# Storing split weights once and loading the parts again in the dense streams of a decoder trunk

## The chip, the cores and the metric

The kernel runs on one core of a Trainium2 chip. The metric is device time of one execution in microseconds (us). TensorE (PE) does the matmuls and has two clock levels, 1.2 and 2.4 GHz; VectorE (DVE), ScalarE (ACT) and GpSimd (POOL) do the elementwise work; SyncE (SP) issues nearly all transfers, in order, on one queue that 16 DMA engines serve. Each engine runs its own instructions strictly in the order that was fixed when the program was built.

## The reference

The reference is a decoder trunk of two layers on 2048 tokens of 1024 channels, in float32. Layer 0 mixes tokens with windowed attention, layer 1 with an RWKV-7 recurrence. After each mixer come an output projection and a gated per-layer embedding:

```python
for i in range(DEPTH):
    hn = rms_norm(h, norm_g[i])
    m = swa_sink_mixer(...) if i % 2 == 0 else rwkv7_mixer(...)   # both end in (o * silu(z)) @ w_out
    h = h + m
    h = h + jax.nn.sigmoid(h @ ple_w_gate[i]) * (p[i] @ ple_w_proj[i])
return rms_norm(h, final_norm_g)
```

## The kernel before

To keep float32 accuracy on the matmul path, each operand is split into a rounded part `hi` (ACT, a copy to the type fp32r) and a remainder `lo` (DVE, `src - hi`), by `Trunk.split`. A product is then three matmuls, `hi*hi`, `hi*lo` and `lo*hi` (`mm3`, L567 to L569).

The work is in four phases: `attn_proj` (0 to about 490 us), `attention` (to about 1250), `rwkv_proj` (to about 1985) and `rwkv` (to the end). Beside attention, and beside the recurrence of `rwkv`, runs a dense stream, an object of the class `Dense`. It is a list of jobs (kind, group of 512 tokens), done in order. In attention the jobs are

```python
"00 01 02 03 10 11 o0 g0 o1 l0 g1 o2 l1 g2 o3 l2 g3 12 l3".split()
```

where 00 to 03 and 10 to 12 are the embedding projections p0 and p1 of a group, o the output projection, g the gate and l the low-rank input of the next layer. In `rwkv` they are z0 to z3 (a projection), o0 g0 o1 g1 o2 g2, then p3 o3 g3. A job is cut into units of one weight tile of 128 x 1024 (8 units for o, g and z, 2 for p and l), 86 + 98 = 184 units in all. A unit is 8 steps of 3 matmuls. Between two steps the other work of the phase issues its own instructions, so the stream fills what attention or the recurrence leaves free on TensorE.

For unit u, `w_load` (L110) issues the load of the raw weights, `wraw`, at step 8(u-2), and `w_split` (L120) makes `dwh` on ACT and `dwl` on DVE at step 8(u-1)+4. The matmuls of u begin at step 8u. All these tiles come from one pool, `wp`, with six buffers (L464), so that before the change a unit takes three of them, `wraw`, `dwh` and `dwl`, and two units fit. The same weights come back for every group of tokens: the tile of o0's first unit is loaded and split again for o1, o2 and o3.

The order of the instructions on each engine is not quite that of the code: the program is built with a scheduler that moves instructions by its own timeline (`schedule_with_timeline_sim=True`, L1429).

Of the kernel before, what the change touches and what calls it, by code (L numbers as in the profile page):

```python
# [10 lines left out]
F32R = mybir.dt.float32r  # L11
# [7 lines left out]
KT = C // 128  # L19
# [24 lines left out]
def f32(ap):  # L44
    return ap.bitcast(F32)
# [7 lines left out]
class Dense:  # L53
# [54 lines left out]
        return aux  # L108

    def w_load(self, u):  # L110
        kind, n, c = u
        k = self.kinds[kind]
        kt = k.get("kt", KT)
        m = 128 * KT // kt
        raw = self.tr.wp.tile([128, KT * 128], F32, name="wraw", tag="w4")
        w = k["w"][:, k.get("c0", 0) + c * m:k.get("c0", 0) + (c + 1) * m]
        self.nc.sync.dma_start(out=raw.rearrange("p (k m) -> p k m", m=m), in_=w.rearrange("(k p) m -> p k m", p=128))
        return raw

    def w_split(self, u, raw):  # L120
        hi, lo = (self.tr.wp.tile([128, KT * 128], F32R, name=nm, tag="w4") for nm in ("dwh", "dwl"))
        self.tr.split(hi, lo, raw, scale=self.kinds[u[0]].get("scale"))
        return hi, lo

    def run(self):
        units, begin, events = [], {}, {}

        def at(step, *what):
            events.setdefault(step, []).append(what)

        owner = []
        for j, (kind, n) in enumerate(self.jobs):
            kt = self.kinds[kind].get("kt", KT)
            b = begin[kind, n] = 8 * len(units)
            units += [(kind, n, c) for c in range(self.kinds[kind].get("units", kt))]
            for k in range(kt):
                free = owner[len(owner) - KT] if len(owner) >= KT else -99
                if "after" in self.kinds[kind]:

                    fill = max(free + 1, begin[self.kinds[kind]["after"], n] + 8 * k + 8)  # L140
                else:
                    fill = max(free, b + k - 9) + 3
                    pre = 3 if "pre" in self.kinds[kind] else 0
                    if pre:
                        at(fill - pre, "pre", j, k)
                    at(fill - pre - self.lead, "fetch", j, k)
                assert fill <= b + k
                at(fill, "fill", j, k)
                if (kind, n) == self.late:
                    at(max(fill, b), "late", j, k)  # L150
                owner.append(8 * len(units) - kt + k)
        for u in range(len(units)):
            at(8 * (u - 2), "w_load", u, None)
            at(8 * (u - 1) + 4, "w_split", u, None)
            for ct in range(KT if "aux" in self.kinds[units[u][0]] and not units[u][2] else 0):
                at(8 * (u + ct) - 4, "aux", units[u][:2], ct)
        raws, tiles, wraw, ws, auxs = {}, {}, {}, {}, {}
        job = -1
        first = -16
        assert first <= min(events)  # L160
        yield
        for s in range(first, 8 * len(units)):
            self.left = 8 * len(units) - s
            for what, a, k in sorted(events.pop(s, []), key=lambda e: ("fetch", "w_load", "fill", "pre", "aux", "w_split", "late").index(e[0])):
                if what == "fetch":
                    kind, n = self.jobs[a]
                    kd = self.kinds[kind]
                    while not kd.get("ready", lambda n, k: True)(n, k):
                        yield
                    raws[a, k] = kd["fetch"](n, k)  # L170
                elif what == "fill":
                    kind, n = self.jobs[a]
                    tiles[a, k] = self.kinds[kind].get("fill", self.fill)(n, k, raws.pop((a, k), None))
                elif what == "pre":
                    kind, n = self.jobs[a]
                    raws[a, k] = self.kinds[kind]["pre"](n, k, raws[a, k])
                elif what == "aux":
                    auxs[a, k] = self.kinds[a[0]]["aux"](a[1], k)
                elif what == "late":
                    while self.rest is None:  # L180
                        yield
                    self.tr.split(*(x[:, G - self.rest.shape[2]:] for x in tiles[a, k]), self.rest[:, k])
                elif what == "w_load":
                    wraw[a] = self.w_load(units[a])
                else:
                    ws[a] = self.w_split(units[a], wraw.pop(a))
            if s >= 0:
                u, i = divmod(s, 8)
                kind, n, c = units[u]
                kd = self.kinds[kind]  # L190
                kt = kd.get("kt", KT)
                k, ct = i % kt, c * (KT // kt) + i // kt
                if k == 0:
                    if ct == 0:
                        job += 1
                    ps = self.mp.tile([128, G], F32, name="ps")
                hi, lo = ws[u]
                m = KT // kt * 128
                sl = slice(k * m + (ct % (KT // kt)) * 128, k * m + (ct % (KT // kt)) * 128 + 128)
                self.tr.mm3(ps, hi[:, sl], lo[:, sl], *tiles[job, k], k == 0, k == kt - 1)  # L200
                if k == kt - 1:
                    self.tr.start(kd["evac"](n, ct, ps, tiles[job, ct] if kt == KT else None, auxs.pop(((kind, n), ct), None)))
                    self.cols_done[kind, n] = ct + 1
            yield
# [1228 lines left out]
```

## Time and profile before

| | us |
|---|---|
| median of 3 runs | 3120.83 (3119.34 to 3126.83) |
| the profiled execution | 3124.84, its span 3123.0 |
| PE busy | 2885.0 (92% of the span) |
| DVE busy | 2112.2 (68%) |
| ACT busy | 1438.3 (46%) |
| POOL busy | 1023.5 (33%) |

The span is the time from the first to the last instruction of the profiled execution. An engine's busy time is the union of its instructions; its idle time costs something only where it stands on the way to the end. The transfers moved 532.87 MB, at a mean of 171 GB/s.

### The profile page before, as it was taken

The numbers are of one execution on the slowest core, as the hardware profiler recorded it, in microseconds if no ns is written. First come the engines' busy times: TensorE is split into PE (matmuls) and PEld (weight loads), VectorE is DVE, ScalarE is ACT, GpSimd is POOL, SyncE is SP. The second block draws the span as 40 slices with busy tenths as digits, with TensorE's granted clock in tenths as the row PEclk, the third lists the DMA queues.
The fourth block names the chain that finished last, engine by engine and source line by source line (L and its number), as shares of the span: only waits on it lengthen the run. The fifth ranks groups of instructions, "written<-read, shape, count | busy, mean of one in ns | idle before, by whom it ended". The sixth has DMA issues, their size and how long they took to land. (4 is left out here: it accounts for less than half of the span.)

```text
span 3123.0 us, 56427 instructions
## 1 busy us (share of the span) xinstructions
PE 2885.0 (92%) x21416; PEld 2284.2 (73%) x21416; DVE 2112.2 (68%) x3665; ACT 1438.3 (46%) x2976; POOL 1023.5 (33%) x886
## 2 busy tenths in 40 slices
PE   7999998999999988898999899988989988989997
PEld 5888886777777766686777688766767766767876
DVE  6532434775888766738678966688795686795555
ACT  5311115874675644626667733433334443443433
POOL 2243500002211232404556700214454435435421
PEclk9999999999999999999999899998899999999999
DMA  7665847985675455636556778855657558568463
GB/s 220 184 142 110 172 131 207 248 210 151 170 189 143 145 172 172 194 115 190 180 185 199 214 210 218 236 150 145 145 150 176 126 143 202 116 150 204 122 192 95
DMA packets 704032, 532.87 MB, mean 171 GB/s; under 512 B 255504, under 2 KB 558736, under 8 KB 703760
## 3 DMA queue, kind: packets, MB, share of 16 engines
q1 hardware_dynamic: 696080, 518.76, 60.3%
q0 software_dynamic: 7680, 10.50, 3.1%
q8 instruction: 169, 2.77, 0.4%
q14 instruction: 103, 0.84, 0.1%
HBM read 350.09 MB, written 168.56 MB: 166 GB/s over the span
## 5 line engine op out<-in xcount | busy, mean ns | idle before, releaser
L567 PE MATMUL ps<-dhi,dwh 128*128 128x512 f32 x1472 | 609.8, 416 | 17.0 <-ACT dwh L516 11.7
L569 PE MATMUL ps<-dhi,dwl 128*128 128x512 f32 x1472 | 595.2, 405 | 26.7 <-DVE dwl L518 15.0
L568 PE MATMUL ps<-dlo,dwh 128*128 128x512 f32 x1472 | 594.3, 405 | 8.3 <-DVE dlo L518 6.1
L567 PE MATMUL ps<-xH,wh 128*128 128x512 f32 x1408 | 556.9, 402 | 25.4 <-DVE kb L1049 10.5
L568 PE MATMUL ps<-xL,wh 128*128 128x512 f32 x1408 | 560.7, 399 | 1.8 <-DVE xL L518 1.1
L569 PE MATMUL ps<-xH,wl 128*128 128x512 f32 x1408 | 561.5, 399 | 0.8 <-DVE wl L518 0.8
L569 PEld LDWEIGHTS ps<-dhi,dwl 128*128 128x128 f32 x1472 | 283.2, 192 | 96.0 <-DVE dwl L518 18.9
L567 PEld LDWEIGHTS ps<-dhi,dwh 128*128 128x128 f32 x1472 | 283.0, 192 | 88.1 <-ACT dwh L516 12.7
L567 PEld LDWEIGHTS ps<-xH,wh 128*128 128x128 f32 x1408 | 269.4, 192 | 88.9 <-DVE kb L1049 14.0
L568 PEld LDWEIGHTS ps<-dlo,dwh 128*128 128x128 f32 x1472 | 283.5, 193 | 67.8 <-DVE dlo L518 8.4
L568 PEld LDWEIGHTS ps<-xL,wh 128*128 128x128 f32 x1408 | 270.8, 192 | 62.3 <-DVE xL L518 2.3
L569 PEld LDWEIGHTS ps<-xH,wl 128*128 128x128 f32 x1408 | 269.9, 192 | 59.3 <-DVE wl L518 1.7
L518 DVE TENSOR_TENSOR dwl<-wraw,dwh 128x1024 fp32r<-128x1024 f32 x152 | 193.8, 1275 | 106.4 <-ACT dwh L516 99.9
L516 ACT ACTIVATE dwh<-wraw 128x1024 fp32r<-128x1024 f32 x152 | 160.5, 1057 | 195.8 <-PE ps L568 122.4
L677 POOL DMA_DIRECT2D t<-t x160 | 126.2, 1272 | 200.2 <-DVE t L674 107.1
L851 ACT ACTIVATE S<-S,nm 128x256 f32<-128x256 f32 (+1 forms) x256 | 125.6, 494 | 65.5 <-DVE nm L848 60.1
L516 ACT ACTIVATE wh<-wr 128x1024 fp32r<-128x1024 f32 x44 | 46.6, 1060 | 188.3 <-DMA wr<-in_attn_w_in 142.9
L518 POOL TENSOR_TENSOR xL<-xs,xH 128x512 fp32r<-128x512 f32 x72 | 111.1, 1554 | 67.7 <-ACT xH L516 67.0
L1247 DVE TENSOR_TENSOR tmp<-P 128x30 f32<-128x30 f32 (+14 forms) x240 | 114.1, 476 | 11.2 <-POOL P L1238 5.2
L842 DVE CUSTOM_DVE_ANT_0 S<-sc,mask,sink 128x256 f32<-128x256 f32 (+1 forms) x256 | 109.0, 469 | 17.6 <-PE sc L838 17.5
L953 DVE SCALAR_TENSOR_TENSOR xs<-hp,mu,xs 128x512 f32<-128x512 f32 x96 | 95.3, 1004 | 29.5 <-ACT xs L952 29.1
L1249 DVE TENSOR_TENSOR P<-P,tmp 128x30 f32<-128x30 f32 (+14 forms) x240 | 110.1, 459 | 6.5
(258 smaller groups left out, 5341.6 us busy)
## 6 DMA issues: line engine op xcount, KB each, us to landing
wraw<-in_ple_w_gate SPq DMA_DIRECT2D x64, 512.0 KB, 4.3
hp<-hn SPq DMA_DIRECT2D x72, 256.5 KB, 4.0
sz<-th SPq DMA_DIRECT2D x64, 256.0 KB, 4.3
ple<-pt SPq DMA_DIRECT2D x64, 256.0 KB, 5.9
wraw<-in_attn_w_out SPq DMA_DIRECT2D x32, 512.0 KB, 4.4
aux<-ple SPq DMA_DIRECT2D x64, 256.0 KB, 3.9
yd<-kx SPq DMA_DIRECT2D x32, 512.0 KB, 4.5
wraw<-in_rwkv_w_in SPq DMA_DIRECT2D x32, 512.0 KB, 4.8
```

What stands on the lines that cost most here:

```text
L516: nc.scalar.activation(hi, src, AF.Copy)
L518: e.tensor_tensor(out=lo, in0=src, in1=f32(hi), op=ALU.subtract)
L567: mm(ps, lhsT=wh, rhs=ah, start=first, stop=False)
L568: mm(ps, lhsT=wh, rhs=al, start=False, stop=False)
L569: mm(ps, lhsT=wl, rhs=ah, start=False, stop=last)
L677: nc.gpsimd.dma_start(out=t1[32 * d:32 * d + 32, :], in_=t2[32 * a:32 * a + 32, :], accum_op=ALU.add)
L842: nc.vector.tensor_tensor_reduce(out=S[:, i, c0:], in0=sc[:, eo, c0:], in1=mask[:, c0:], scale=1.0, scalar=sink[:, 4 * g + 2 * j + eo:4 * ...
L851: nc.scalar.activation(S[:, i, c0:], S[:, i, c0:], AF.Exp, bias=nm[:, i:i + 1], accum_out=den[:, i:i + 1])
L953: nc.vector.scalar_tensor_tensor(out=src, in0=t[:, :G], scalar=mus[:, c, k:k + 1], in1=src, op0=ALU.mult, op1=ALU.add)
L1247: nc.vector.tensor_tensor(out=t, in0=P[:, 0:r, r:r + 1].broadcast_to([128, r, n]), in1=P[:, r:r + 1, r + 1:].broadcast_to([128, r, n]), op ...
L1249: nc.vector.tensor_tensor(out=P[:, 0:r, r + 1:], in0=P[:, 0:r, r + 1:], in1=t, op=ALU.add)
```

## The change

A kind's first group of tokens in a stage still loads the raw tile and splits it. If the kind comes again in that stage, the two parts are then written to a memory tensor, `wp_<stream><kind><unit>`, two transfers of 512 KB. Every later group loads the two parts straight into `dwh` and `dwl`, two transfers of 512 KB each instead of one of the raw tile, and does no split. The loads of the parts are issued where the raw load was, at step 8(u-2), and such a unit takes two of the six buffers instead of three, from step 8(u-2) on.

```diff
     def w_load(self, u):
+
         kind, n, c = u
         k = self.kinds[kind]
+        if n != self.first[kind]:
+            return self.w_parts(u)
         kt = k.get("kt", KT)
...
+    def w_parts(self, u):
+        hl = tuple(self.tr.wp.tile([128, KT * 128], F32R, name=nm, tag="w4") for nm in ("dwh", "dwl"))
+        for a, t in enumerate(hl):
+            self.nc.sync.dma_start(out=f32(t), in_=self.parts(u)[a])
+        return hl
+
+    def parts(self, u):
+
+        return self.tr.dram(f"wp_{self.name}{u[0]}{u[2]}", [2, 128, KT * 128])
+
     def w_split(self, u, raw):
+        if u[1] != self.first[u[0]]:
+            return raw
         hi, lo = (self.tr.wp.tile([128, KT * 128], F32R, name=nm, tag="w4") for nm in ("dwh", "dwl"))
         self.tr.split(hi, lo, raw, scale=self.kinds[u[0]].get("scale"))
+        if self.again[u[0]]:
+            for a, t in enumerate((hi, lo)):
+                self.nc.sync.dma_start(out=self.parts(u)[a], in_=f32(t))
         return hi, lo
 
     def run(self):
         units, begin, events = [], {}, {}
+        self.first, self.again = {}, {}
+        for kind, n in self.jobs:
+            self.again[kind] = kind in self.first
+            self.first.setdefault(kind, n)
```

Places in the changed file stand 22 lines further down (L538 and L540 are the split, L120 the raw load, L126 the load of the parts, L140 their store).

Three places show what the scheduler makes of it. The first is ScalarE at the end of the attention phase, where the last units of o3 meet the first projection of the next phase (`xs` and `xH` are inputs of that projection, `dwh` the weights of o3). Before:

```order
L952 ACTIVATE xs<-hp,omu 128x512 x3
L516 ACTIVATE xH_10039<-xs 128x512
L516 ACTIVATE xH_10041<-xs 128x512
L516 ACTIVATE l2h<-l_11558 128x256
L516 ACTIVATE dwh<-wraw 128x1024
L516 ACTIVATE xH_10043<-xs 128x512
L952 ACTIVATE xs<-hp,omu 128x512 x2
L516 ACTIVATE dwh<-wraw 128x1024
```

and after:

```order
L974 ACTIVATE xs<-hp,omu 128x512 x3
L538 ACTIVATE xH_10035<-xs 128x512
L538 ACTIVATE xH_10037<-xs 128x512
L538 ACTIVATE l2h<-l_11496 128x256
L538 ACTIVATE xH_10039<-xs 128x512
L974 ACTIVATE xs<-hp,omu 128x512 x2
L538 ACTIVATE xH_10041<-xs 128x512
```

The splits of o3's weights, which stood behind `xs`, are gone, and the rest keeps its order.

The second is SyncE in the job z0 (`sz` stores a result of z0, `x`, `xa`, `ag`, `uv` and `bvt` feed the recurrence, `aux` and `gnb` are wanted much later). Before:

```order
L284 DMA sz_17918<-th 128x512
L117 DMA wraw<-in_rwkv_w_in 128x8x128
L1341 DMA bvt<-bv 128x8x64
L1195 DMA xa<-ad 128x8x128
L1290 DMA ag<-ab 128x8x256
L1195 DMA xa<-rd 128x8x128
L106 DMA aux<-h_3625 128x512
L117 DMA wraw<-in_rwkv_w_in 128x8x128
L106 DMA aux<-h_3625 128x512 x6
```

and after:

```order
L140 DMA wp_wz_18269<-dwh 128x1024
L140 DMA wp_wz_18269<-dwl 128x1024
L306 DMA sz_17856<-th 128x512
L120 DMA wraw<-in_rwkv_w_in 128x8x128
L1363 DMA bvt<-bv 128x8x64
L1217 DMA xa<-ad 128x8x128
L140 DMA wp_wz_18339<-dwh 128x1024
L1312 DMA ag<-ab 128x8x256
L1217 DMA xa<-rd 128x8x128
L140 DMA wp_wz_18339<-dwl 128x1024
L120 DMA wraw<-in_rwkv_w_in 128x8x128
L106 DMA aux<-h_3625 128x512 x4
```

Two stores now stand ahead of each raw load of the job.

The third is ScalarE in the same job (`th` is the tanh that takes a finished unit's result out, `bn` and `r` belong to the recurrence, `dhi` is a data operand). Before:

```order
L282 ACTIVATE th<-ps 128x512
L516 ACTIVATE dwh<-wraw 128x1024 x2
L282 ACTIVATE th<-ps 128x512
L516 ACTIVATE dwh<-wraw 128x1024
L282 ACTIVATE th<-ps 128x512
L516 ACTIVATE dhi<-xs 128x512
```

and after:

```order
L304 ACTIVATE th<-ps 128x512
L538 ACTIVATE dwh<-wraw 128x1024
L1331 COPY r_18845<-r1p 128x512
L304 ACTIVATE th<-ps 128x512
L538 ACTIVATE dwh<-wraw 128x1024
L304 ACTIVATE th<-ps 128x512
L538 ACTIVATE dwh<-wraw 128x1024 x2
```

The first split shown after is that of z0's fifth unit. The next two, of the sixth and the seventh unit, stand behind the tanh of the unit just before them; before the change the tanh ahead of a split here was that of an earlier unit.

## Rows read from the trace of the kernel before

**Rows 1.** The page's first part: busy time, share of the span, instructions.

```profile
PE 2885.0 (92%) x21416; PEld 2284.2 (73%) x21416; DVE 2112.2 (68%) x3665; ACT 1438.3 (46%) x2976; POOL 1023.5 (33%) x886
```

**Rows 2.** Groups by line: busy us, mean ns, idle before, releasers.

```profile
L567 PE MATMUL ps<-dhi,dwh 128*128 128x512 f32 x1472 | 609.8, 416 | 17.0 <-ACT dwh L516 11.7 <-ACT dhi L516 1.6 <-ACT th L408 1.5
L569 PE MATMUL ps<-dhi,dwl 128*128 128x512 f32 x1472 | 595.2, 405 | 26.7 <-DVE dwl L518 15.0 <-DVE dwl L514 11.7
...
L518 DVE TENSOR_TENSOR dwl<-wraw,dwh 128x1024 fp32r<-128x1024 f32 x152 | 193.8, 1275 | 106.4 <-ACT dwh L516 99.9 <-ACT pt L231 2.9 <-PE ps L569 1.6
L516 ACT ACTIVATE dwh<-wraw 128x1024 fp32r<-128x1024 f32 x152 | 160.5, 1057 | 195.8 <-PE ps L568 122.4 <-DMA wraw<-in_rwkv_w_in 20.2 <-issue 14.5
...
L514 DVE SCALAR_TENSOR_TENSOR dwl<-wraw,dwh 128x1024 fp32r<-128x1024 f32 x32 | 41.8, 1305 | 12.1 <-ACT dwh L513 11.9 <-DMA uv<-vn 0.2
```

**Rows 3.** Windows: stretch, its length, busy by engine, PEclk, DMA share, GB/s.

```profile
480.00:700.00 220.00, 199.95 (x1145) 154.89 (x1144) 147.51 (x556) 155.71 (x471) 5.21 (x4) 0.93 0.87 231
700.00:1100.00 400.00, 398.46 (x2068) 307.68 (x2067) 310.80 (x713) 237.80 (x569) 86.78 (x65) 1.00 0.57 158
1985.00:2060.00 75.00, 66.72 (x368) 50.64 (x368) 52.37 (x90) 26.50 (x41) 14.64 (x14) 1.00 0.88 231
2060.00:2900.00 840.00, 754.02 (x10078) 600.36 (x10078) 641.60 (x975) 331.84 (x661) 381.83 (x314) 0.95 0.64 154
```

**Rows 4.** The waits of PE, 1100 to 1300 us: total us, times, longest.

```profile
PE ps L567 <- ACT dwh L516: 6.2, 1, 6.2
...
PE ps L569 <- DVE dwl L518: 4.8, 2, 3.0
```

**Rows 5.** ACT in order of time from 1102 us: start us, us.

```profile
1102.09 0.72 ACT L952 ACTIVATE xs<-hp,omu 128x512 f32<-128x512 f32 x1 [2.52 <-DMA hp<-hn]
1104.62 0.72 ACT L952 ACTIVATE xs<-hp,omu 128x512 f32<-128x512 f32 x1 [1.80 <-DMA hp<-hn]
...
1107.67 1.04 ACT L516 ACTIVATE dwh<-wraw 128x1024 fp32r<-128x1024 f32 x1
```

**Rows 6.** PE in order of time from 3003 us.

```profile
3003.47 0.40 PE L568 MATMUL ps<-dlo,dwh 128*128 128x512 f32 x1
3008.78 0.80 PE L569 MATMUL ps<-dhi,dwl 128*128 128x512 f32 x1 [4.91 <-DVE dwl L514]
3009.38 0.63 PE L567 MATMUL ps<-dhi,dwh 128*128 128x512 f32 x1
3009.80 0.63 PE L568 MATMUL ps<-dlo,dwh 128*128 128x512 f32 x1
...
3013.43 0.39 PE L568 MATMUL ps<-dlo,dwh 128*128 128x512 f32 x1
3013.66 0.40 PE L569 MATMUL ps<-dhi,dwl 128*128 128x512 f32 x1
```

**Rows 7.** The waits of PE, 2060 to 2900 us.

```profile
PE y L1334 <- DVE uv L1320: 15.6, 7, 4.9
PE ps L399 <- DVE th L305: 14.4, 7, 5.6
PE aps L1208 <- DVE tt L1282: 10.1, 4, 3.3
PE ps L569 <- DVE dwl L514: 6.8, 3, 2.8
PE ps L569 <- DVE dwl L518: 6.2, 4, 3.3
```

**Rows 8.** Windows of the tile dwl alone: PE, PEld and DVE, clock, DMA.

```profile
2060.00:2900.00 840.00, 205.16 (x498) 96.90 (x497) 81.38 (x63) 0.95 0.64 154
```

**Rows 9.** All waits, 1985 to 2060 us.

```profile
ACT dwh L516 <- DMA wraw<-in_rwkv_w_in: 16.3, 4, 4.8
...
PE ps L569 <- DVE dwl L518: 4.0, 3, 1.8
```

**Rows 10.** Transfers: the queue (packets, MB, share), issues (KB, us to landing).

```profile
q1 hardware_dynamic: 696080, 518.76, 60.3%
...
wraw<-in_ple_w_gate SPq DMA_DIRECT2D x64, 512.0 KB, 4.3
...
wraw<-in_rwkv_w_in SPq DMA_DIRECT2D x32, 512.0 KB, 4.8
```

## The prediction

> **What bounds the kernel now.** I began with the page's busy times: TensorE is busy 92% of the span [rows 1], so about 238 us are left to win, and no more than what of them stands on splits. The groups by line come next [rows 2]: the dense stream's matmuls waited 11.7 us for `dwh` and 15.0 + 11.7 us for `dwl`, 38 us that name a weight split outright. DVE and ACT spend 1.28 and 1.06 us on each. The windows tell where that matters [rows 3]. From 700 to 1100 us TensorE is busy 398.5 of 400 us: nothing to win. In the recurrence, 2060 to 2900, it idles 86 us, and the granted clock is 0.95, so a tenth of the stretch ran at 1.2 GHz. In z0, 1985 to 2060, the transfers are the busiest thing, at 0.88.
>
> What a single wait looks like is seen at 1102 us [rows 4, 5]: ACT works in order, `xs` waits there for a transfer, the split of o3's third unit stands behind it, and TensorE waits 6.2 us; 4.8 us more for `dwl` follow. At 3003 us it waits 4.91 us for `dwl`, and after that its matmuls stand 0.42 us apart for some ten of them, against 0.23 when the clock is back at 2.4 GHz [rows 6]: another 1.9 us for the clock.
>
> **What goes.** Of 184 units the first use keeps its split: 22 in attention (p0 2, p1 2, o 8, g 8, l 2), 26 in the second stream (z 8, o 8, g 8, p 2). The other 136 lose it: 136 x (1.06 + 1.28) = 318 us of work, nearly all of which stands beside TensorE's own work and is worth nothing by itself. Two things are worth something.
>
> First, the named waits of the two tails, where TensorE has nothing else to do: 6.2 + 4.8 [rows 4] and 4.9 us [rows 6], 15.9 in all, and by the last place's 1.9 us some 5 us for the clock after the three longer gaps. Those units get parts, so I credit 21. If the inputs that stand on the same ACT queue were late next at 1102, half of that place's 11 us and of its clock loss would stay, and the sum would be some 13.
>
> Second, the recurrence. Its two `dwl` rows sum to 13.0 us [rows 7]. Of the 63 `dwl` that fall in the stretch [rows 8], 16 (o0 and g0) are first uses, so 47/63 of it, 10 us, can go. The three largest other waits for DVE, 15.6 + 14.4 + 10.1 = 40 us in 18 waits [rows 7], shrink too, as 47 x 1.29 = 61 us leave a DVE that is busy 641.6 us. Lower end: in that proportion, 4 us. Upper end: one split ahead of each wait, 18 x 1.28 = 23 us. I take 11, nearer the middle than either, since in 7 of 25 listed waits it was the split itself that was late. Of 21 us I keep three quarters, 16, because the next thing in DVE's queue is then late instead. The clock: a tenth of 840 us at 1.2 GHz, with matmuls 0.42 instead of 0.23 us apart, cost at most 38 us; with 16 of 86 us of idle time gone, a fifth of that would be 7, and I take 5. Together 21, with ends of 5 and 43.
>
> **What comes.** The parts' loads add one transfer to each of 136 units, and the stores two to each of 46 (p3 is not stored): 228 x 0.524 MB = 120 MB on a queue of 519 MB [rows 10]. No row shows these transfers, so I price them by a crowded stretch: z0 moved 231 GB/s at a share of 0.88 [rows 3], which is 3.8 us of all 16 engines per MB, 2.0 us per transfer. By the Trainium skill, "DMA: Bandwidth & Descriptors", section "Anatomy of one DMA — SWDGE (gpsimd) path", a transfer has a fixed cost of about 2 us and a variable one of bytes/436e9 s; that would be an estimate of 2.3 us per MB, and the z0 stores below would come to 19 instead of 32 us. The row is dearer, and the sum goes by the row.
>
> A part's load waits on SP for the last matmul of unit u-3, whose buffers it takes; two whole units, 48 matmuls x 0.23 = 11 us, are left to land in. Such transfers landed in 4.3 to 4.8 us [rows 10], and a raw load had less room, so I cost this at 0. Behind the waiting load on SP stand result stores and inputs of the attention or the recurrence, which are also asked for ahead of time. If the cover goes, it goes in the tails, where units follow each other without a break: 32 units (o3 and g3 of both streams) at half a microsecond, 15 us, is the upper end. From 700 to 1100 a share of 0.57 leaves 172 us free, and all stores there are hidden.
>
> z0: 16 stores, 8.4 MB, take 32 us of the engines in a stretch with 0.12 x 75 = 9 us free. Four of its splits already waited 16.3 us for their raw load [rows 9], and the order now puts two stores ahead of each such load. Upper end 23 us, lower end 0, as the stretch behind has a share of 0.64 and takes what is not urgent; I take 7. On ACT the splits of the sixth and seventh unit stand behind the tanh of the unit before, so TensorE waits for a split each time: at most 2 x (1.06 + 1.28) = 4.7 us. Three waits of that kind, 4.0 us, were there before [rows 9], and I take 3 more.
>
> The start of attention, 480 to 700: 8 stores and 8 further loads of p0 and p1, and 8 stores for the first units of o0, 12.6 MB, 47 us of the engines, and 0.13 x 220 = 29 us are free. Upper end 18, lower 0; 5 taken, since the loads that attention needs first are asked for ahead.
>
> The second unit of p0 and of p3 takes its `dwl` buffer from the unit just before it, so its split runs when that unit ends: 2 x 1.28 less the matmuls that need only `dwh`, 2 us.
>
> **The sum.** 21 + 21 less 7 + 3 + 5 + 2 = 25 us less. The profiled execution took 3124.84 us with a span of 3123.0, so its successor should take 3100; it stood 4 us above the median of the runs, 3120.83, and from that median the forecast is 3096.
>
> **Rivals.**
> (a) Nothing to be seen. ACT and DVE are idle half and a third of the span [rows 1]; in the recurrence each wait that goes is replaced by the next thing late on the same queues, so its 21 us don't come, and the tails' 21 are spent on the 17 us of cost: 4 us less, 3117. For it: 398.5 of 400 us busy from 700 on. Against it: the 4.91 us at 3003 stand in a tail with nothing else. The Trainium skill, "Perfetto Trace Analysis", section "Identifying the Most-Contended Engine", says to improve the most contended engine first; by that rule the change works on the wrong engines. Here the idle time of the contended engine names the split in 38 us, so the trace agrees with the rule only in part.
> (b) Slower: the stores crowd the queue in front of the raw loads wherever a kind is used first. Each of the 46 stored units brings 2 x 2.0 = 4.0 us of DMA time, and the raw load of the next but one unit stands behind it on the same queue. Against 42 us won, this decides the sign once a first-use unit is on average 0.9 us longer; at 1.4 us it is 64 us, and the time 3143. For it: z0's splits wait for loads now [rows 9], and 480 to 700 is at 0.87. Against it: g0 and most of o0 of the first stream run at 0.57, and o0 and g0 of the second at 0.64 [rows 3].
> (c) A larger gain: DVE's relief goes through in full, 43 us in the recurrence, and the stores are hidden but for the split's own 5 us: 21 + 43 - 5 = 59, 3062.
> That the parts are not loaded as written is not a rival: the built order has them in place of the splits.
>
> **From this the numbers.** Forecast (10 to 45 us less) 0.50, (c) 0.16, (a) 0.18, (b) 0.16. The runs differ by up to 0.24%, so 0.3%, 9 us, is about what can be told from no change. Faster 0.66, same 0.18, slower 0.16. The forecast's own range is 3076 to 3111; to hold 8 in 10 it has to reach (c)'s edge and some way into (b): 3062 to 3134. The dear ends all at once, 64 us of cost against 18 won, would be 3167; that takes four places at once, and the range leaves it out.
>
> **What would show it.** `dwh` and `dwl` on ACT and DVE 48 times each; the queue at 638 MB; no wait for `dwl` at o3 of either stream, and TensorE at 2.4 GHz through both tails; from 2060 to 2900 idle time of 65 to 75 us; z0 at a share near 1.0 and 8 to 12 us longer. I would be wrong if the recurrence idles as before although DVE has 60 us less to do, if TensorE's waits name the parts' transfers, or if o0 and g0 of either stream stretch.

## The result, and the profile after

The changed kernel takes 3074.9 us (median of 4 runs, 3069.91 to 3078.94) against 3120.9 of the kernel before beside it: a ratio of 0.9844, interval 0.9829 to 0.986. That is 46 us by the medians and 49 by the ratio, where 25 were forecast. The profiled execution has a span of 3070.6 us, 52.4 less than before.

The page's first part of the changed kernel, to be read beside [rows 1]:

```profile
PE 2865.7 (93%) x21416; PEld 2265.5 (74%) x21416; DVE 1950.4 (64%) x3529; ACT 1314.0 (43%) x2840; POOL 1005.2 (33%) x886
```

TensorE issues as many instructions as before and is busy 19.3 us less; it idles 3070.6 - 2865.7 = 204.9 us against 238.0. So the 52.4 us are 33.1 of idle time and 19.3 of matmuls that ran shorter. DVE lost 161.8 us of work and ACT 124.3.

The groups by line of the changed kernel (busy us, mean ns, idle before, what ended it), beside [rows 2]; every line stands 22 higher:

```profile
L589 PE MATMUL ps<-dhi,dwh 128*128 128x512 f32 x1472 | 610.1, 416 | 23.4 <-ACT dwh L538 9.9 <-ACT dhi L538 5.6 <-DVE aux L264 4.1
L591 PE MATMUL ps<-dhi,dwl 128*128 128x512 f32 x1472 | 590.6, 402 | 11.5 <-DVE dwl L540 11.0 <-DMA dwl<-wp_ao 0.5
...
L540 DVE TENSOR_TENSOR dwl<-wraw,dwh 128x1024 fp32r<-128x1024 f32 x40 | 49.3, 1232 | 36.2 <-ACT dwh L538 28.8 <-PE ps L590 4.1 <-DMA wp_ag<-dwh 3.0
L538 ACT ACTIVATE dwh<-wraw 128x1024 fp32r<-128x1024 f32 x40 | 42.3, 1057 | 54.7 <-PE ps L590 29.6 <-DMA wraw<-in_rwkv_w_in 8.9 <-DMA wraw<-in_attn_w_out 4.1
...
L536 DVE SCALAR_TENSOR_TENSOR dwl<-wraw,dwh 128x1024 fp32r<-128x1024 f32 x8 | 10.1, 1259 | 2.5 <-ACT dwh L535 2.5
```

The splits are there 40 + 8 = 48 times. The right-hand columns matter as much as the counts. In [rows 2] ACT had stood idle 195.8 us ahead of L516, 122.4 of it until TensorE freed the buffer that `dwh` takes; behind an instruction that stands, everything else on ACT stands too. Now it is 54.7 us. DVE's idle time ahead of its splits fell from 118.5 us to 38.7. So each queue was given back the splits' work and the time it stood at them; per split the standing is no shorter than before (on ACT 195.8 us for 152, now 54.7 for 40).

The windows of the changed kernel, with the borders of [rows 3]:

```profile
480.00:700.00 220.00, 205.05 (x1217) 158.37 (x1216) 144.90 (x570) 155.80 (x479) 5.17 (x4) 0.98 0.98 288
700.00:1100.00 400.00, 395.94 (x2028) 308.63 (x2026) 275.13 (x668) 208.17 (x529) 92.90 (x74) 0.99 0.78 251
...
1985.00:2060.00 75.00, 61.99 (x594) 46.37 (x592) 61.21 (x111) 22.09 (x39) 14.96 (x15) 0.91 0.94 301
2060.00:2900.00 840.00, 778.25 (x10334) 617.01 (x10334) 586.63 (x929) 302.16 (x657) 394.38 (x331) 0.96 0.77 209
```

The transfers are at 0.98 from 480 to 700, and yet TensorE does more there than before (205.05 against 199.95 us). From 2060 to 2900 it idles 61.8 us, not 86. It is busy for less than before from 700 to 1100 (395.94 against 398.46) and from 1985 to 2060 (61.99 against 66.72).

Such windows no longer hold the same work, as the changed kernel is ahead: its z0 begins at 1955.6 us and not at 1985.2. The start times of the same matmuls in both traces cut the span into stretches that do (us; single executions):

| stretch | before | changed |
|---|---|---|
| up to the first matmul of the first dense stream | 490.0 | 488.5 |
| from there to the first matmul of o3 | 598.6 | 586.2 |
| o3 | 62.1 | 53.3 |
| the rest of this stream (l2, g3, 12, l3) | 96.3 | 89.1 |
| from its last matmul to the first of z0 (`rwkv_proj`) | 738.2 | 738.5 |
| z0 | 61.0 | 81.4 |
| from z1 to the last `y`, a matmul of the recurrence | 934.4 | 892.2 |
| the rest | 142.4 | 141.4 |

Three things in it were not to be seen in the windows. The changed kernel is 13.9 us ahead before o3 begins (1074.7 us, before 1088.6). z0 is 20.4 us longer, and more than that comes back behind it. The last tail is hardly shorter. From z0's first matmul to the last `y` TensorE idles 77.5 us, before 94.3, for the same number of matmuls (11,398 and 11,397).

TensorE's waits in the changed kernel, from 1060 to 1260 us (the place of [rows 4]); from 2060 to 2900 (beside [rows 7]); and from 2900 on (total us, times, longest):

```profile
PE ps L589 <- DVE aux L264: 4.1, 1, 4.1
...
PE ps L589 <- ACT dhi L538: 2.4, 1, 2.4
...
PE ps L589 <- DMA dwh<-wp_ao: 0.6, 1, 0.6
PE ps L591 <- DMA dwl<-wp_ao: 0.5, 1, 0.5
```

```profile
PE y L1356 <- DVE uv L1342: 19.7, 8, 5.2
PE ps L421 <- DVE th L327: 8.1, 5, 2.6
PE wq L1290 <- DVE at L1277: 6.5, 1, 6.5
...
PE ps L591 <- DVE dwl L540: 1.6, 1, 1.6
```

```profile
PE ps L591 <- DVE dwl L540: 6.4, 1, 6.4
```

At o3 of attention the 6.2 + 4.8 us for the split are gone, and 4.1 for `aux` stand there instead; the 2.4 for `dhi` fall at l3, at 1202.6 us. The 4.1 have the cause that the 6.2 had [rows 5]: three `xs` stand ahead, on ACT and then on DVE, and wait for the transfer of `hp`:

```profile
1086.66 2.08 ACT L974 ACTIVATE xs<-hp,omu 128x512 f32<-128x512 f32 x3 [4.28 <-DMA hp<-hn]
```

So it is the next thing on the same queues. In the recurrence `dwl` went from 13.0 to 1.6 us and `th` from 14.4 to 8.1, while `uv` rose. The 6.4 us at the end are the split of p3's second unit: DVE does it at 2952.8 us, 7 us after p3's first unit has ended, behind six instructions `res` that take it 7.25 us. The parts' own transfers cost TensorE 1.1 us.

The queue and two landings (KB, us), beside [rows 10]:

```profile
q1 hardware_dynamic: 614736, 638.31, 69.8%
...
dwh<-wp_ao SPq DMA_DIRECT2D x24, 512.0 KB, 6.1
dwl<-wp_ao SPq DMA_DIRECT2D x24, 512.0 KB, 6.8
```

120 MB more, in fewer packets.

### The profile page after: what moved, and what is told of

Its sections match the earlier page's. It is cut to its first block, busy times and chain, and to the rows that moved or that the text cites. A ratio compares the mean times of both kernels' runs of the same rounds, so it can differ in the third digit from the quotient of the medians.

```text
span 3070.6 us, 56425 instructions
## 1 busy us (share of the span) xinstructions
PE 2865.7 (93%) x21416; PEld 2265.5 (74%) x21416; DVE 1950.4 (64%) x3529; ACT 1314.0 (43%) x2840; POOL 1005.2 (33%) x886
## 3 DMA queue, kind: packets, MB, share of 16 engines
q1 hardware_dynamic: 614736, 638.31, 69.8%
## 5 line engine op out<-in xcount | busy, mean ns | idle before, releaser
L589 PEld LDWEIGHTS ps<-dhi,dwh 128*128 128x128 f32 x1472 | 281.1, 191 | 95.5 <-ACT dwh L538 11.4
L590 PEld LDWEIGHTS ps<-dlo,dwh 128*128 128x128 f32 x1472 | 281.8, 192 | 61.8 <-DVE dlo L540 4.5
L591 PEld LDWEIGHTS ps<-xH,wl 128*128 128x128 f32 x1408 | 269.0, 191 | 59.2 <-DVE wl L540 2.6
L540 POOL TENSOR_TENSOR xL<-xs,xH 128x512 fp32r<-128x512 f32 x72 | 109.8, 1535 | 76.0 <-ACT xH L538 73.0
L538 ACT ACTIVATE wh<-wr 128x1024 fp32r<-128x1024 f32 x44 | 46.6, 1059 | 190.9 <-DMA wr<-in_attn_w_in 144.9
L1052 POOL TENSOR_TENSOR kb<-kb,mhalf 128x16 f32<-128x16 f32 x32 | 100.6, 3146 | 36.9 <-DVE kb L1051 36.6
L540 POOL TENSOR_TENSOR dlo<-z,dhi 128x512 fp32r<-128x512 f32 x16 | 22.3, 1408 | 258.8 <-ACT dhi L538 252.2
```

The lines of the kernel that those rows point to most:

```text
L538: nc.scalar.activation(hi, src, AF.Copy)
L540: e.tensor_tensor(out=lo, in0=src, in1=f32(hi), op=ALU.subtract)
L589: mm(ps, lhsT=wh, rhs=ah, start=first, stop=False)
L590: mm(ps, lhsT=wh, rhs=al, start=False, stop=False)
L591: mm(ps, lhsT=wl, rhs=ah, start=False, stop=last)
L1052: nc.gpsimd.tensor_tensor(out=bs[:, :, 0], in0=bs[:, :, 0], in1=self.mhalf.broadcast_to([128, m]), op=ALU.pow)
```

## The experiments

Differences are worked out from each ratio, at 3.12 us for 0.1%; by them the changed kernel is 49 us (44 to 53) faster than the kernel before. Except where said otherwise, edits are made to the changed kernel.

**1 and 2. One stream alone.** The first has `self.name == "w"`, the second `self.name == "a"`; the guard in `w_load` and `w_split` asks for `self.again` too.

```diff
-            self.again[kind] = kind in self.first
+            self.again[kind] = kind in self.first and self.name == "w"
...
-        if n != self.first[kind]:
+        if self.again[kind] and n != self.first[kind]:
```

> Parts in the second stream alone (z, o, g of the rwkv layer); the first stream splits every unit as before. In the changed kernel's trace the second stream starts 30 us earlier than before and the kernel ends 52 us earlier, so if the two streams' gains simply add, this one wins 17 to 23 us: about 3100. By the prediction's terms (21 in the recurrence and 4.9 with its clock in the last tail, less 7 + 3 in z0 and some for p3) it is 3105. Rival, that the second stream's gain was only possible because the first stream ended early and moved the transfers: no gain, 3115 to 3125.

> Parts in the first stream alone (p0, p1, o, g, l of attention); the second stream splits every unit as before. If the gains add, the 30 us that the changed kernel was ahead at z0 stay to the end: about 3091. By the prediction's terms (16 in the tail at o3 with its clock, less 5 at the start) it is 3110. Rival, that the lead is lost again because the second stream waits for something else than the dense weights: 3105 to 3121.

Measured: the second stream alone 3098.44 us, ratio 0.9913 (0.9894 to 0.9932), 27 us; the first alone 3104.15 us, 0.9932 (0.9913 to 0.9952), 21 us. The two are 48 us together, and the changed kernel has 49: the gains add, and neither stream lives on the other's. The first stream's lead is not lost, but it is not the full 30 us that the changed kernel's trace had at the start of z0: in its own trace it is 25 us there and 17 at the end.

**3. z left out.** `kind != "z"` in the same line, with the same guard.

> As the changed kernel, but z is split at every use, so z0 stores nothing and z1 to z3 load raw weights. Theory 1, that z0's stores cost about 10 us and z1 to z3 win them back: within 5 us of the changed kernel, 3070 to 3080. Theory 2, that z0's stores cost the 36 us by which z2 starts later against z0, and that the 37 us won back by z3 would have come without z's parts: faster than the changed kernel, 3045 to 3065. Theory 3, that z's parts in the recurrence are worth more than the stores: slower, 3085 to 3100.

Measured: 3092.2 us, 0.9891 (0.9872 to 0.991), 34 us. Theory 3: z's parts are worth 15 us in all, stores of z0 included. A slow z0 is a good bargain.

**4. The stores alone.** The kernel before, with the stores after each first split:

```diff
         self.tr.split(hi, lo, raw, scale=self.kinds[u[0]].get("scale"))
+        if self.again[u[0]] and u[1] == self.first[u[0]]:
+            for a, t in enumerate((hi, lo)):
+                self.nc.sync.dma_start(out=self.parts(u)[a], in_=f32(t))
```

> The kernel before with the 46 units' stores added, and nothing loaded as parts: every unit is split. Theory 1 (the prediction's terms of 5 at the start of attention and 7 in z0): 12 us slower, 3133. Theory 2, the stores crowd every first use (1.4 us a unit): 3185. Theory 3, stores are hidden: within 5 us of before, 3116 to 3126, and then what slows z0 in the changed kernel is not the stores.

Measured: 3125.21 us, 1.0001 (0.9987 to 1.0016): the stores cost nothing that can be measured. In the traces, TensorE's matmuls on `dwh` (busy, count, then clock, share and GB/s of the whole window), first of the kernel before, then with the stores alone:

```profile
1985.00:2060.00 75.00, 48.59 (x147) 1.00 0.88 231
2060.00:2160.00 100.00, 44.51 (x129) 0.91 0.48 131
2160.00:2290.00 130.00, 42.61 (x119) 0.92 0.65 157
```

```profile
1985.00:2060.00 75.00, 40.69 (x115) 0.90 1.02 301
2060.00:2160.00 100.00, 44.10 (x126) 0.94 0.60 160
2160.00:2290.00 130.00, 53.78 (x152) 0.91 0.67 161
```

z0 does lose: the dense stream has done 241 of these matmuls by 2160 us, against 276. By 2290 it is 393 against 395. But TensorE as a whole is not behind. All that it did, of the kernel before, then with the stores alone:

```profile
1985.00:2060.00 75.00, 66.72 (x368) 50.64 (x368) 52.37 (x90) 26.50 (x41) 14.64 (x14) 1.00 0.88 231
2060.00:2160.00 100.00, 84.68 (x1001) 67.30 (x1000) 85.25 (x131) 32.59 (x55) 36.86 (x31) 0.91 0.48 131
```

```profile
1985.00:2060.00 75.00, 61.38 (x416) 46.43 (x414) 43.80 (x86) 21.22 (x33) 10.85 (x12) 0.90 1.02 301
2060.00:2160.00 100.00, 94.69 (x1277) 74.56 (x1276) 89.92 (x151) 39.35 (x70) 36.23 (x32) 0.94 0.60 160
```

By 2160 it has done 1693 matmuls with the stores against 1369 without, by 2290 3169 against 3164. As TensorE keeps its built order, the order itself is another here: more of the recurrence stands ahead of z0's matmuls. By the stretches of the table z0 is 20.6 us longer with the stores, and from z1 to the last `y` 19.6 us are won back. How much of z0's lag is this exchange and how much the crowded queue is not shown; TensorE idles 5.3 us more up to 2060 and 10.0 us less in the 100 us after it.

**5. The work put back, without TensorE waiting for it.** Each unit loaded as parts also copies and subtracts into a third buffer that nobody reads:

```diff
         if u[1] != self.first[u[0]]:
+            idle = self.tr.wp.tile([128, KT * 128], F32, name="wraw", tag="w4")
+            self.nc.scalar.activation(idle, f32(raw[0]), AF.Copy)
+            self.nc.vector.tensor_tensor(out=idle, in0=f32(raw[1]), in1=idle, op=ALU.subtract)
             return raw
```

> As the changed kernel, but for each unit loaded as parts ACT and DVE also do a copy and a subtraction of the split's size into a third buffer that nobody reads: the splits' 2.3 us of engine work and the three buffers a unit are back, TensorE doesn't wait for them. Theory 1 (the prediction: the tails' gain is the direct wait, the recurrence's gain is DVE's relief): the tails' 20 us stay and the recurrence's are lost, 3090 to 3105. Theory 2, all of the gain is the wait for the split itself, as engines had time enough: 3070 to 3082. Theory 3, all of it is relief of the engines or the room of two instead of three buffers a unit: 3115 to 3125.

Measured: 3118.2 us, 0.9986 (0.9972 to 0.9999): 4 of the 49 us are left. Theory 3 by its number. The rows of the added work, and TensorE's windows at o3 of attention, of the kernel before, the changed one and this one, in that order:

```profile
L137 DVE TENSOR_TENSOR wraw<-dwl,wraw 128x1024 f32<-128x1024 f32 x136 | 175.6, 1291 | 71.9 <-ACT wraw L136 61.8 <-DMA dwh<-wp_ao 3.7 <-DMA h<-hh 2.3
L136 ACT ACTIVATE wraw<-dwh 128x1024 f32<-128x1024 f32 x136 | 143.7, 1057 | 147.3 <-PE ps L593 92.3 <-issue 26.1 <-DVE wraw L137 18.1
```

```profile
1060.00:1250.00 190.00, 168.00 (x698) 132.90 (x697) 124.87 (x141) 87.94 (x134) 61.28 (x50) 0.94 0.54 168
```

```profile
1060.00:1250.00 190.00, 177.66 (x741) 140.85 (x739) 111.51 (x134) 83.22 (x137) 68.84 (x59) 0.96 0.76 248
```

```profile
1060.00:1250.00 190.00, 172.36 (x704) 137.08 (x703) 127.00 (x142) 93.33 (x142) 59.70 (x51) 0.94 0.76 240
```

TensorE's waits there, with the work put back:

```profile
PE ps L592 <- DVE aux L267: 7.6, 2, 5.2
PE ps L592 <- ACT dhi L541: 3.7, 1, 3.7
PE ps L250 <- ACT hh L323: 3.5, 1, 3.5
```

No wait for a weight is among them, and yet the place has lost more than half of its gain; o3 takes 59.2 us, between the 53.3 of the changed kernel and the 62.1 of before. Of the 11 us that [rows 4] gave to the split, 7.6 stand now at `aux`; `hh` and `dhi` follow later, at 1205.5 and 1226.3 us. The longest, 5.2 us, has the old cause again, in this run's trace:

```profile
1098.39 0.72 ACT L977 ACTIVATE xs<-hp,omu 128x512 f32<-128x512 f32 x1 [2.71 <-DMA hp<-hn]
1099.21 0.75 DVE L978 SCALAR_TENSOR_TENSOR xs<-hp,mu,xs 128x512 f32<-128x512 f32 x1 [4.08 <-ACT xs L977]
```

The name in a row of waits was that of the last in the queue: none of the added work stands right ahead of this `aux`, and no row names what the added work cost here.

**6. The room alone.** The third buffer without the work:

```diff
         if u[1] != self.first[u[0]]:
+            idle = self.tr.wp.tile([128, KT * 128], F32, name="wraw", tag="w4")
+            self.nc.gpsimd.memset(idle[:, 0:1], 0.0)
             return raw
```

> As the changed kernel, but each unit loaded as parts also takes a third buffer of the pool, in which GpSimd sets one column: no work of ACT or DVE is back, the parts' loads wait for the end of unit u-2 and not u-3, as in the run with the work put back (3118). Theory 1, that run lost 43 us because of the engines' work: this one stays near the changed kernel, 3072 to 3082. Theory 2, it lost them because the loads stand on SP for a unit longer and all that is queued behind them comes late: 3105 to 3120. Between the two both count.

Measured: 3082.26 us, 0.9869 (0.9852 to 0.9886), 41 us: 8 are lost, between the theories' numbers but far nearer the first. SP's queue shows that the loads of half of the units (67 of 136) wait here for GpSimd's column, where in run 5 they waited for DVE's subtraction, so the expectation's "end of unit u-2" holds only for some:

```profile
SPq L126 <- POOL wraw L136: 161.4, 67, 6.8
```

The room is then some 8 of the 45 us that run 5 lost (the intervals of this run and of the changed kernel overlap, so it may be nothing), and the other 37 need the work. By the stretches of the table run 5 takes longer than the changed kernel by 9.8 us up to o3, 5.9 in o3, 7.7 behind it, 1.8 in z0, 16.2 from z1 to the last `y` and 4.2 in the rest; this run by 2.0, -0.4, -0.5, 1.8, 4.1 and 1.0. One way in which the work can cost is not separated: in run 5 the subtraction also holds the third buffer, and the weights' loads stand 500 us on SP's queue, against 320 in the changed kernel and 354 here.

**7 and 8. The work of one engine put back,** with two buffers a unit and a small scratch tile, 896 of the 1024 columns. For ACT, and in its place for DVE:

```diff
+        self.idle = tr.pool(es, name + "di", 1, side=side).tile([128, 896], mybir.dt.bfloat16, name="idle")
...
         if u[1] != self.first[u[0]]:
+            self.nc.scalar.activation(self.idle, f32(raw[0])[:, 0:896], AF.Copy)
```

```diff
+            self.nc.vector.tensor_tensor(out=self.idle, in0=f32(raw[1])[:, 0:896], in1=f32(raw[0])[:, 0:896], op=ALU.subtract)
```

> As the changed kernel, with two buffers a unit, but ACT makes a copy of 896 of the 1024 columns of the high part of each unit loaded as parts into a scratch tile that nobody reads (about 0.95 us, 136 times; 128 columns less than the split's). Theory 1a (the prediction: DVE's relief is what counts in the recurrence, ACT's only at o3 of the first stream): 3078 to 3086. Theory 1b, ACT's queue holds back as much as its share of the work: 3088 to 3098. Theory 2, room alone: 3072 to 3079.

> As the changed kernel, with two buffers a unit, but DVE subtracts 896 of the 1024 columns of the parts of each unit loaded as parts into a scratch tile that nobody reads (about 1.15 us, 136 times). Theory 1a (the prediction): most of the engines' share is here, 3095 to 3108. Theory 1b, the two engines share it: 3088 to 3098. Theory 2, room alone: 3072 to 3079.

Measured: with ACT's work 3101.03 us, 0.993 (0.9915 to 0.9944), 22 us faster than before, so 27 lost. With DVE's 3135.74 us, 1.004 (1.0027 to 1.0054): 61 lost, and slower than the kernel before. Both miss their ranges. The groups of the added instructions, ACT's, then DVE's:

```profile
L136 ACT ACTIVATE idle<-dwh 128x896 bf16<-128x896 f32 x136 | 129.1, 949 | 303.3 <-DMA dwh<-wp_wz 86.8 <-DMA dwh<-wp_wg 62.1 <-DMA dwh<-wp_wo 57.2
```

```profile
L136 DVE TENSOR_TENSOR idle<-dwl,dwh 128x896 bf16<-128x896 f32 x136 | 160.5, 1180 | 146.4 <-DMA dwl<-wp_wo 39.7 <-DMA dwl<-wp_ag 36.8 <-DMA dwl<-wp_wg 23.3
```

Each queue now works and also stands, 303 and 146 us, mostly until a part's transfer lands. That DVE's loss is over twice ACT's fits the prediction's order of the two, and ACT bears 303 us of standing for 27. But the losses don't add (27 + 61 against 45 with both), and in run 5 DVE stood 71.9 us and mostly for ACT. So it may be that an instruction on DVE that stands in order for a transfer is dearer than its work; these two runs don't give the price of the work by itself. They do show a loss without a third buffer, with the weights' loads standing no longer on SP's queue (314 and 303 us) than in the changed kernel.

**9 and 10. Half of the parts.** Raw weights and one part are loaded; the other part is still computed. For the high part (the low one likewise, with ACT's copy in place of the subtraction; the scaled subtraction isn't shown):

```diff
+            hi = self.tr.wp.tile([128, KT * 128], F32R, name="dwh", tag="w4")
+            self.nc.sync.dma_start(out=f32(hi), in_=self.parts(u)[0])
+            return raw, hi
...
+            raw, hi = raw
+            lo = self.tr.wp.tile([128, KT * 128], F32R, name="dwl", tag="w4")
...
+                self.nc.vector.tensor_tensor(out=lo, in0=raw, in1=f32(hi), op=ALU.subtract)
+            return hi, lo
```

> Raw weights and the high part are loaded for the later uses, DVE still subtracts for the low part: as many transfers as in the changed kernel, ACT relieved, DVE not, three buffers a unit. By the prediction ACT's share is the 6.2 us at o3 of the first stream and some of the clock's loss; DVE's queue stays as it was: 3108 to 3116. Theory 2, ACT's queue is the one that matters (the copy stands behind evacuations and the recurrence's copies): 3085 to 3100. Theory 3, transfers or buffers cost something here: over 3124.

> Raw weights and the low part are loaded for the later uses, ACT still copies for the high part: DVE relieved, ACT not, three buffers a unit. By the prediction DVE's share is most of it (4.8 us at o3, 4.9 in the last tail, 16 in the recurrence, some clock): 3085 to 3097. Theory 2, ACT's copy is as often the late one: 3100 to 3112. If the two halves are far below the 46 us together, either part being late is enough to stop TensorE, or the room in the buffers matters.

Measured: 3182.99 us, 1.0196 (1.0178 to 1.0215), and 3156.48 us, 1.0109 (1.0089 to 1.0129): 61 and 34 us slower than before, with less work on an engine and the changed kernel's number of transfers. Theory 3 in the first; in the second no range, but the expectation's last sentence, a part that is late or the room in the buffers. TensorE's first row of waits in each:

```profile
PE ps L600 <- DVE dwl L143: 35.1, 31, 8.8
```

```profile
PE ps L595 <- ACT dwh L140: 36.3, 44, 4.8
```

TensorE now waits for the half split directly, for `dwl` 51.5 us with the 16.4 of the scaled ones, where [rows 2] have 26.7, and three times as long for `dwh` as the 11.7 there. The traces also say why the half split is late. The groups of the half split, DVE's and ACT's:

```profile
L143 DVE TENSOR_TENSOR dwl<-wraw,dwh 128x1024 fp32r<-128x1024 f32 x112 | 146.7, 1311 | 103.0 <-PE ps L599 98.8 <-DMA h<-hh 3.1 <-DMA xa<-rd 0.7
L140 ACT ACTIVATE dwh<-wraw 128x1024 fp32r<-128x1024 f32 x136 | 143.6, 1056 | 212.7 <-PE ps L596 132.7 <-issue 75.8 <-DMA dwl<-wp_ag 1.4
```

It waits for a matmul of TensorE, which frees its buffer, and hardly for a transfer (for 75.8 us ACT waited for nothing that the profile shows): the loaded part had landed 11 us before it in the median of each run. So both runs were slow for the buffer, at least in the main, and not for the second transfer. They tell nothing of ACT's share against DVE's, for which they were meant.

**11. p3 earlier.**

```diff
-[(kind, n) for n in range(NG) for kind in "pog"[n < NG - 1:]]
+[(kind, NG - 1 if kind == "p" else n) for n in range(NG) for kind in ("pog" if n == 1 else "og")]
```

> As the changed kernel, with the two units of p3 moved from the head of the last tail to ahead of o1, in the middle of the recurrence. The changed kernel waits 6.4 us there for the split of p3's second unit. If TensorE's work ahead of that wait is only moved and the wait is hidden by the recurrence's own matmuls: 5 to 8 us faster than the changed kernel, 3067 to 3070. Rival, that the recurrence loses as much, because it has less of the dense stream left to fill its last waits, or that the next thing is late at o3: 3072 to 3080.

Measured: 3071.14 us, 0.9834 (0.9816 to 0.9852), 52 us. No wait for `dwl` is left from 2900 us on, and 1.7 us of one stand in the recurrence. The median is the lowest of all, but its interval overlaps that of the changed kernel: not told apart.

**12. First splits with GpSimd,** and p3 earlier.

```diff
-        self.tr.split(hi, lo, raw, scale=self.kinds[u[0]].get("scale"))
+        self.tr.split(hi, lo, raw, lo_engine="pool", scale=self.kinds[u[0]].get("scale"))
```

> p3's units ahead of o1, as in the run with p3 earlier (3071), and the low part of the first uses is subtracted by GpSimd, not by DVE, where no scale stands in the way: some 38 more subtractions, about 49 us, leave DVE, mostly in attention and z0. If relief of DVE is worth about what it was worth in the change (46 us for 318 us of both engines' work, so about 0.15 us each): 7 us faster than with p3 earlier, 3064. Rival, GpSimd takes about twice as long for each and TensorE waits for the low part at each first use: 3080 to 3100.

Measured: 3098.11 us, 0.9922 (0.9908 to 0.9937), 24 us: 27 worse than run 11, the rival. The group of the split and TensorE's wait:

```profile
L540 POOL TENSOR_TENSOR dwl<-wraw,dwh 128x1024 fp32r<-128x1024 f32 x40 | 96.2, 2406 | 381.3 <-ACT dwh L538 165.2 <-DMA ple<-pt 109.1 <-PE ps L591 57.5
```

```profile
PE ps L591 <- POOL dwl L540: 12.0, 6, 6.0
```

It takes 2.41 us where DVE takes 1.23, and GpSimd stood 165 us for ACT at it. 49 us less on DVE were worth less than that.

## Why the prediction was right, and what was off

The direction was right, and so was it that both streams gain: the first gives 21 us, where the prediction's terms come to 11 (16 for o3 with its clock, less 5 at the start), and the second 27, where they come to 16 (21 in the recurrence and 5 in the last tail, less 7 + 3 in z0). The size was not: 49 us lie between the forecast's 25 and rival (c)'s 59, and the median of 3074.9 lies just below the forecast's own range of 3076 to 3111 and inside the wide one, 3062 to 3134.

**The losses were mis-sized.** 7 + 3 for z0, 5 for the start of attention and 2 for p0 and p3 came to 17. Run 4 puts the stores at 0, within 5 us either way. The local reading of z0 was right: TensorE's waits for z0's splits are 12.9 us in the changed kernel and 12.1 with the stores alone, before 2.2, so 10 us more, as forecast. The step that failed took a stretch's loss for the kernel's: z0 is some 20 us longer, not 8 to 12, and in run 4 as much comes back behind it, at least in part because the order was only exchanged. At the start of attention nothing was lost: the way to o3 got shorter, as is told below. p3's wait is 6.4 us and not about 1, for DVE's queue and not for the buffer that the prediction named, and run 11 doesn't show that it costs that much in the end.

**The price was mis-sized too.** 3.8 us of all 16 engines per MB was the busy share of z0 divided by its bytes. By the queue's share of the span, the stores alone added 125 us (64.3% of 3123.7 less 60.3% of 3123.0) for 48.2 MB, 2.6 us per MB, and the whole change 260 us (69.8% of 3070.6) for 119.6 MB net, 2.2. By the Trainium skill, "DMA: Bandwidth & Descriptors", section "Anatomy of one DMA — SWDGE (gpsimd) path", an estimate from bytes was 2.3, and the measurement agrees with that better than with the row I chose. That section is about transfers that GpSimd issues; those here are SP's. On the queue of before a packet carried 745 bytes on average (518.76 MB in 696,080, [rows 10]); the stores' are larger, as 48.2 MB came in 13,248 packets more (709,328 of the stores alone).

**The tails' 21 came for another reason and in another place.** The prediction took the 15.9 us of named waits as worth their length because TensorE waited for the split itself. o3 is 8.8 us shorter and the last tail 1.0. Run 5 has no wait for a split at o3 and yet loses more than half of o3's gain, which run 6 with the room alone keeps (52.9 us). So what was won there has to do with the engines' work, which the prediction counted for the recurrence alone. For o3 it kept "if the inputs that stand on the same ACT queue were late next" as a lower end: such inputs, `xs`, were the cause before and still are, for 4.1 us in the changed kernel.

The larger part lies where the prediction had a loss of 5 us and "nothing to win". From the first dense matmul to o3's, over 480 to 1075 us, the changed kernel is 12.4 us shorter for the same 3129 matmuls, and behind o3 it wins 7.2 more. From 480 to 700 TensorE did 1217 matmuls instead of 1145, at a granted clock of 0.98 instead of 0.93. Run 5 has the clock too (0.98, 1208 matmuls) but only 2.6 of the 12.4 us by o3. Why is not shown.

**The recurrence** was right in kind and size. From z0's first matmul to the last `y` TensorE idles 16.8 us less and is busy 5.0 less, where 16 and 5 were forecast, though z0's loss is inside these numbers and was to be taken off. From 2060 to 2900 the idle time is 61.8 us, below the 65 to 75 foretold, with `dwl` down by 11.4 of the 13.0 us and DVE's work by 55 us, not 61. The ends of 5 and 43 stand in the prediction without their sum. Run 5 took nearly all of the gain away with the engines' work and the room. The prediction counted 318 us of work and let stand unread, in the same rows of [rows 2], the 195.8 and 118.5 us for which ACT and DVE stood at the splits.

**The clock.** 5 + 5 us were counted; TensorE's busy time fell 19.3 us with the same number of instructions, so this term was small by about half. That both tails would run at 2.4 GHz throughout was wrong: the granted clock from 1060 to 1250 is 0.96, up from 0.94, and behind the last `y` 0.92, before 0.93.

**The parts' landing** at 0 held: 1.1 us of waits, with landings of 6 to 7 us for o's parts in the first stream where 4.3 to 4.8 had been assumed, inside the 11 us of two units. (Its upper end, 32 units at half a microsecond, is 16 us and not 15.)

**The rivals.** (a) would have the recurrence's gain spent on the next thing in the queue, and the tails' on the costs; runs 1 and 2 each show a gain by itself. (b) falls with run 4. (c) had the right idea, that the stores are hidden, and put 43 us on the recurrence where the second stream gave 27 in all.

**What stays open.** Of the 45 us of run 5, some 8 are room; how the rest divides between work, standing and buffers that are held longer, and between ACT and DVE, is not settled, since runs 7 and 8 made the queues stand for transfers. Each kernel's instructions are also placed anew among the others when it is built; run 4's changed order and unchanged time speak against an effect of that alone, but it wasn't tried by itself.

## What to carry to other kernels

Work that is repeated for each group of tokens can be worth storing even when the queue is busy 60% and the engines that do the work are idle for a third and half of the span: read not only an instruction's busy time but the idle time ahead of it, because on a queue that works in order all that follows stands too. That idle time is no price, though: 303 us of it on ACT went with 27 us lost, 146 on DVE with 61. A stretch that gets slower need not make the kernel slower: compare what all streams have done at a later mark, between the same instructions and not between fixed times, before charging for it. And a wait's name is the last thing in a queue; look further up the queue before crediting its length. With one part loaded and the other computed the kernel was slower than with none, but here mainly because the computed part waited for its buffer, so that is no price of mixing the two.

## What the runs showed of the hardware

The kernel's main queue moved 23% more bytes in 12% fewer packets (638.31 MB in 614,736, before 518.76 MB in 696,080), and its engines' time rose only from 60.3% of 3123.0 us to 69.8% of 3070.6, 14%: the parts, stored in the order in which they are used, came cheaper by the byte than what the kernel moved before.

The same subtraction of 128x1024 took 2.41 us with GpSimd and 1.23 with DVE.

ACT was idle 303 us ahead of its added instruction, and the kernel lost 27 us; DVE was idle 146 us ahead of its own, and the kernel lost 61.
